# A written-down order for ScalarE, VectorE and GpSimd in the up phase of a decoder trunk

## The chip, the core and the metric

The kernel runs on one core of a Trainium2 chip. The metric is the device time of one execution in microseconds (us). The engines are PE (TensorE), ACT (ScalarE), DVE (VectorE), POOL (GpSimd) and SP (SyncE, which here only issues transfers). Each engine works through its own list of instructions in the list's order; an instruction whose inputs are not there holds up all that stand behind it.

## The reference

Two layers; each has a mixer and then an MLP. The change lies in the MLP, of which this is the whole (all float32, 1024 positions, width 1024, `D_FF` 4096):

```python
h = rms_norm(x, norm2[l])
x = x + jnp.square(jax.nn.relu(h @ w_up[l])) @ w_down[l]
```

## The kernel before, in words

Positions lie along the free axis in two halves of 512 (`c` 1 and 0), channels along the 128 partitions. A float32 operand is split into a high part, rounded to `fp32r` (`split`: a cast on ACT, line 131), and a low rest (a subtraction on DVE, line 132); each product is three matmuls of 128x512 (`mm3`, lines 219, 224, 225).

Both matrix products of the MLP use a Winograd form of Strassen's scheme on 2x2 blocks: 7 block products in place of 8. The table `STEPS` names them in order; the operands are sums of blocks, and the results are sums of products that gather in PSUM:

```python
STEPS = (
    ("X", 0, "A11", "B11"), ("Y", 0, "A12", "B21"), ("X", 1, "S2", "T2"), ("Z", 0, "S1", "T1"),
    ("X", 2, "S3", "T3"), ("Z", 1, "S4", "B22"), ("X", 3, "A22", "T4"),
)
```

The **up phase** (before: lines 931 to 1025) runs 16 times per layer (`fp`), each time over two tiles of 128 hidden channels; such a time is called a round here. A round has the seven steps 0 to 6; a step is 12 matmuls (4 pairs of input tiles, three each). Bank X takes four products one after the other, bank Z two, bank Y one.

Around the steps of a round, three kinds of work stand on the other engines:

- **Results.** After X0, X1 and Z0 ACT copies the bank to SBUF (`keep`, line 952: P1, U2, P5); the next product into the same bank may only start when that copy is done. DVE then forms each hidden block from those (B11 after step 1, line 998; B22 after step 4, line 1006; B12 after step 5, line 1010; B21 straight from PSUM after step 6), with a ReLU and the scale of the RMS norm (line 957). POOL squares it (line 960). B11 and B21 are split in two and stored; DVE forms T1 to T4 (line 972) from the blocks, which are stored whole.
- **The next round's weights** (`weight_steps`, lines 780 to 825). SP loads two tiles of 128x1024, a top and a low one, into the two buffers `raw` (line 801). The top one is split to A11 and A12. POOL forms s1 and s2 (lines 809, 810) into the tile `s`, which is split to S1 and S2; then s3 (line 818, split to S3), and s4, written into the low tile (line 820), which is split to S4 and A22. So the low buffer comes free for the next load only when that last split (`vh`, `vl`) is done. The split tiles have two buffers for `w` (A11 with A12, S1 with S2, in turn), and one each for `u` (S3) and `v` (S4 with A22).
- **Stores** of the hidden blocks to DRAM, issued by SP.

The kernel records all this in program order, and a scheduler then sets the order of each engine's list by priority and by its own idea of when things are ready; the results' work is recorded with a raised priority (`early(EVAC_EARLY)`). The 12 matmuls of a step are held in order by order-only dependences (`pace`). The **down phase** (from line 1050) has the same steps for `w_down`, and takes its weights by the same function.

Of the kernel before, what the change touches and what calls it, by code (L numbers as in the profile page):

```python
# [79 lines left out]
def trunk_kernel(tc, xT, w_in, w_out, w_up, w_down, pool_w, sgw, sgb, sgn, cst, outT):  # L80
# [8 lines left out]
    with ExitStack() as ctx:  # L89
# [23 lines left out]
        def tmp():  # L113
            return t512("tmp", 4)
# [12 lines left out]
        def early(n):  # L127
            return tc.high_priority(offset=n)

        def split(hi, lo, src):  # L130
            nc.scalar.copy(hi, src)  # L131
            nc.vector.tensor_sub(lo, src, hi.bitcast(F32))  # L132

        def xt(part, k, c, dt=F32R):

# [167 lines left out]
        for l in range(DEPTH):  # L303
# [476 lines left out]
            def weight_steps(srcs, n, out):  # L780

                turns = "p (n k w) -> p k n w"
                r = {}

                def room(tag, names, pool, bufs, by=None):
                    two = [
                        pool.tile([P, CH * len(names)], F32R, tag=tag + x, name=nm(tag + x), bufs=bufs) for x in "hl"
                    ]  # L790
                    for i, b in enumerate(names):
                        out[b] = tuple(
                            t.rearrange(by or "p (k n w) -> p k n w", n=n, k=len(names))[:, i] for t in two
                        )
# [10 lines left out]
                def top():  # L805
                    split(*room("w", ("A11", "A12"), per, 2, turns), r["top"])
                    s12 = r["s12"] = ex.tile([P, D], F32, tag="s", name=nm("s12"), bufs=1)
                    s1, s2 = (s12[:, i * CH : (i + 1) * CH].rearrange("p (n w) -> p n w", n=n) for i in range(2))
                    nc.gpsimd.tensor_add(s1, r["a2"][:, 0], r["a2"][:, 1])  # L809
                    nc.gpsimd.tensor_sub(s2, s1, r["a1"][:, 0])  # L810
                    r["s2"] = s2

                def sums():
                    split(*room("w", ("S1", "S2"), per, 2), r["s12"])

                def third():
                    s3 = tmp()
                    nc.gpsimd.tensor_sub(s3.rearrange("p (n w) -> p n w", n=n), r["a1"][:, 0], r["a2"][:, 0])
                    split(*room("u", ("S3",), mw, 1), s3)
                    nc.gpsimd.tensor_sub(r["a2"][:, 0], r["s2"], r["a1"][:, 1])  # L820

                def low():
                    split(*room("v", ("S4", "A22"), mw, 1, turns), r["low"])

                return {0: load, 2: top, 3: sums, 4: third, 6: low}

            def up_blocks(fp):

# [85 lines left out]
            def load_block(fp, b):  # L914

                h, lo = block_tiles(b)
                if b in STORED:
                    nc.sync.dma_start(h.bitcast(F32), hid[fp, b + "h"])
                    nc.sync.dma_start(lo.bitcast(F32), hid[fp, b + "l"])
                else:  # L920
                    raw = t512("hr", 4, F32, mw)
                    nc.sync.dma_start(raw, hid[fp, b])
                    split(h, lo, raw)
                return h, lo

            a_next = {}
            for _, step in sorted(weight_steps(*up_blocks(0), a_next).items()):
                step()


            with tc.tile_pool(name=f"mu{l}", bufs=1, reuse_waits="tile") as mu:

                rms_done = False

                def ct(dt=F32):
                    return t512("ct", 10, dt, mu)

                for fp in range(NFP):
                    a, a_next = a_next, {}
                    steps_w = weight_steps(*(up_blocks(fp + 1) if fp < NFP - 1 else down_blocks(0, 0)), a_next)  # L940
# [8 lines left out]

                    def keep(ps):  # L950
                        t = ct()
                        nc.scalar.copy(t, ps)  # L952
                        return t

                    def hidden(b, src, t, c):

                        nc.vector.scalar_tensor_tensor(  # L957
                            out=t, in0=src, scalar=0.0, in1=rbc[c], op0=ALU.max, op1=ALU.mult
                        )
                        nc.gpsimd.tensor_mul(t, t, t)  # L960
                        hb[b] = t
                        if b in STORED:
                            parts = [ct(F32R) for _ in range(2)]
                            split(*parts, t)
                            for x, part in zip("hl", parts):
                                nc.sync.dma_start(hid[fp, b + x], part.bitcast(F32))
                        elif classic or b != "B12":
                            nc.sync.dma_start(hid[fp, b], t)

                    def mixed(b, x, y, op):  # L970
                        t = ct()
                        op(t, hb[x], hb[y])  # L972
                        hb[b] = t
                        nc.sync.dma_start(hid[fp, b], t)

# [9 lines left out]
                    for step in range(len(STEPS)):  # L985
                        bank, i = products(a, xb, banks, step, 0)
                        ps = banks[bank]
                        if step == 3 and fp == 0:
                            rms(1, 0)
                            rms_done = True  # L990
                            for f, args in later:
                                f(*args)
                        with early(EVAC_EARLY):
                            if (bank, i) == ("X", 0):
                                kept["P1"] = keep(ps)
                            elif bank == "Y":
                                t = kept["P1"]
                                nc.vector.tensor_add(t, ps, t)
                                after_rms(hidden, "B11", t, t, 1)
                            elif (bank, i) == ("X", 1):  # L1000
                                kept["U2"] = keep(ps)
                            elif (bank, i) == ("Z", 0):
                                kept["P5"] = keep(ps)
                            elif (bank, i) == ("X", 2):
                                t = kept["P5"]
                                nc.vector.tensor_sub(t, ps, t)
                                hidden("B22", t, t, 0)
                            elif (bank, i) == ("Z", 1):
                                t = kept["U2"]
                                nc.vector.tensor_sub(t, t, ps)  # L1010
                                hidden("B12", t, t, 0)
                                if not classic:
                                    mixed("T1", "B11", "B12", nc.vector.tensor_sub)
                                    mixed("T2", "B22", "T1", nc.vector.tensor_add)
                                    mixed("T3", "B22", "B12", nc.vector.tensor_sub)
                            else:
                                hidden("B21", ps, ct(), 1)
                                if not classic:
# [31 lines left out]
            with tc.tile_pool(name=f"md{l}", bufs=1, reuse_waits="tile") as md:  # L1050
# [13 lines left out]
                for g in range(n_groups):  # L1064
                    bs, b_next = b_next, [{}, {}]
                    for u in range(2):
                        a, a_next, steps_w = a_next, {}, {}
                        if u == 0:
                            steps_w = weight_steps(*down_blocks(g, 1), a_next)
                        elif g < n_groups - 1:  # L1070
                            steps_w = weight_steps(*down_blocks(g + 1, 0), a_next)
                        banks = [{"X": pso(), "Y": psj(), "Z": psg()} for _ in range(2)]
                        for step in range(len(STEPS)):
                            for q in range(2):
# [3 lines left out]
                                with early(EVAC_EARLY):  # L1078
# [14 lines left out]
                            if step in steps_w:  # L1093
                                steps_w[step]()
# [125 lines left out]
```

## Time and profile before

| | |
|---|---|
| median of 3 runs (lowest to highest) | 2456.49 us (2449.84 to 2456.86) |
| the profiled execution: its own time | 2451.93 us |
| its span (first to last instruction) | 2450.2 us |
| mean granted clock of TensorE | 0.953 of full |
| up phase, first layer | about 505 to 905 us of the span |
| up phase, second layer | about 1709 to 2110 us |
| chain that ended last, by engine | PE 52%, DVE 14%, POOL 14%, issue 10%, DMA 5%, ACT 4% |

Times in the profile are counted from the span's start. A timeline row has the start, the duration, the engine, the line, the operation with the tile written and the tiles read, and in brackets the idle time of the engine before it with what ended that idle time. Matmuls overlap: the distance from one start to the next is what one costs, not its duration. On DVE and ACT, too, an instruction starts up to 0.1 us before the one ahead has its end recorded, so a run of them is read from start to start.

### The profile page before, as it was taken

To read this page: it belongs to the slowest core of one execution; us is meant where nothing else is said; L and a number is where in the kernel's file an instruction comes from. 1 tells how busy PE (TensorE), PEld (TensorE's weight loads), DVE (VectorE), ACT (ScalarE), POOL (GpSimd) and SP (SyncE) were. 2 spreads that over 40 slices of the span, in tenths; PEclk is the share of its full clock that TensorE was granted. 3 is DMA by queue.
4 is the path that set the end of the run, shared out by engine and by line. 5 is a ranking of instruction groups with operands and counts; after the bars stand their busy time and mean duration, and the time that the engine had idled before them with its cause. 6 is when DMAs were issued, how large, how long until landed. Compare 5 with 4: busy or idle time off the path is not lost.

```text
span 2450.2 us, 30479 instructions
## 1 busy us (share of the span) xinstructions
PE 2206.1 (90%) x10480; PEld 1817.2 (74%) x10480; DVE 1824.8 (74%) x2244; ACT 942.3 (38%) x1667; POOL 1263.6 (52%) x1169
## 2 busy tenths in 40 slices
PE   7999899878888889999999898997788888999997
PEld 5988787656666767888788887876666666778786
DVE  8787779956565669888868787798556665898874
ACT  5565553522222233333355665344222222333321
POOL 7676756754444442332367777459444454333315
PEclk9999899989999999999999998998899999999998
DMA  3000102234344367555311010232444343955421
GB/s 121 26 27 27 40 31 95 98 122 151 137 142 138 126 236 252 181 168 159 99 49 44 9 54 14 61 104 99 146 136 135 129 142 135 311 182 177 160 93 69
DMA packets 153739, 283.19 MB, mean 116 GB/s; under 512 B 15088, under 2 KB 48368, under 8 KB 153584
## 3 DMA queue, kind: packets, MB, share of 16 engines
q1 hardware_dynamic: 151920, 279.15, 34.4%
q10 hardware_dynamic: 1664, 2.10, 0.2%
q8 instruction: 82, 1.34, 0.2%
q14 instruction: 73, 0.60, 0.1%
HBM read 190.49 MB, written 90.70 MB: 115 GB/s over the span
## 4 chain that ended last, share of the span: by engine, by line
PE 52%; DVE 14%; POOL 14%; issue 10%; DMA 5%; ACT 4%; SPq 0%; DVEq 0%; POOLq 0%; ACTq 0%
PE po L219 8%; PE po L224 7%; PE po L225 7%; PE pj L219 5%; PE pj L224 5%; PE pj L225 5%; PE pg L219 3%; POOL s L809 3%; PE pg L225 3%; PE pg L224 3%; POOL s L810 3%; DVE s L411 3%; DMA raw<-in_w_up 2%; PE t L432 2%; POOL a L414 1%
## 5 line engine op out<-in xcount | busy, mean ns | idle before, releaser
L960 POOL TENSOR_TENSOR ct<-ct 128x512 f32<-128x512 f32 x128 | 137.9, 1077 | 387.3 <-DVE ct L957 386.3
L809 POOL TENSOR_TENSOR s<-raw 128x512 f32<-128x512 f32 x62 | 112.3, 1811 | 410.5 <-DMA raw<-in_w_down 244.3
L132 DVE TENSOR_TENSOR wl<-raw,wh 128x1024 fp32r<-128x1024 f32 x114 | 168.2, 1475 | 101.7 <-ACT wh L131 101.4
L414 POOL TENSOR_TENSOR a<-a,s 128x255 f32<-128x255 f32 (+1 forms) x192 | 220.6, 1151 | 29.4 <-DVE s L411 22.0
L131 ACT CAST wh<-raw 128x1024 fp32r<-128x1024 f32 x114 | 119.4, 1047 | 239.6 <-PE pj L224 217.1
L219 PE MATMUL pj<-hB,wh 128*128 128x512 f32 x504 | 198.1, 393 | 1.7 <-ACT hB L854 1.7
L224 PE MATMUL pj<-lB,wh 128*128 128x512 f32 x504 | 198.2, 393 | 1.0 <-DVE lB L855 1.0
L225 PE MATMUL pj<-hB,wl 128*128 128x512 f32 x504 | 197.6, 392 | 0.0
L219 PE MATMUL po<-hT,wh 128*128 128x512 f32 x256 | 117.4, 459 | 60.3 <-ACT ct L952 59.5
L411 DVE TENSOR_TENSOR_SCAN s<-s 128x256 f32<-128x256 f32 (+3 forms) x128 | 130.6, 1028 | 54.4 <-POOL s L404 52.8
L219 PE MATMUL po<-hT,uh 128*128 128x512 f32 x248 | 109.7, 442 | 66.1 <-ACT ct L952 62.2
L1056 DVE TENSOR_TENSOR acc<-acc,po 128x512 f32<-128x512 f32 x240 | 158.9, 678 | 11.4 <-PE po L225 10.2
L131 ACT CAST vh<-raw 128x1024 fp32r<-128x1024 f32 x62 | 65.1, 1049 | 233.7 <-PE po L224 172.4
L132 DVE TENSOR_TENSOR ct<-ct,ct 128x512 fp32r<-128x512 f32 x64 | 75.9, 1186 | 82.4 <-ACT ct L131 82.3
L972 DVE TENSOR_TENSOR ct<-ct,ct 128x512 f32<-128x512 f32 x120 | 110.2, 939 | 34.4 <-POOL ct L960 34.4
L131 ACT CAST ct<-ct 128x512 fp32r<-128x512 f32 x64 | 39.4, 615 | 228.3 <-POOL ct L960 228.3
L132 DVE TENSOR_TENSOR wl<-s,wh 128x1024 fp32r<-128x1024 f32 x62 | 83.2, 1341 | 51.9 <-ACT wh L131 51.9
L438 DVE TENSOR_TENSOR tl<-t,th 128x512 fp32r<-128x512 f32 (+1 forms) x160 | 98.1, 626 | 30.8 <-ACT th L436 29.7
L219 PEld LDWEIGHTS po<-hT,wh 128*128 128x128 f32 x256 | 54.8, 214 | 89.4 <-ACT ct L952 71.9
L219 PEld LDWEIGHTS po<-hT,uh 128*128 128x128 f32 x248 | 50.7, 205 | 92.7 <-ACT ct L952 75.3
L131 ACT CAST hT<-hr 128x512 fp32r<-128x512 f32 x122 | 74.0, 620 | 116.9 <-DMA hr<-hd_T 71.6
L400 ACT ACTIVATE s<-z 128x256 f32<-128x256 f32 (+1 forms) x192 | 94.5, 501 | 60.3 <-PE z L396 37.0
(270 smaller groups left out, 7396.6 us busy)
## 6 DMA issues: line engine op xcount, KB each, us to landing
raw<-in_w_up SPq DMA_DIRECT2D x64, 512.0 KB, 3.7
raw<-in_w_down SPq DMA_DIRECT2D x64, 512.0 KB, 3.7
hd_T<-ct SPq DMA_DIRECT2D x120, 256.0 KB, 4.0
hr<-hd_T SPq DMA_DIRECT2D x120, 256.0 KB, 3.3
raw<-in_w_in SPq DMA_DIRECT2D x36, 512.0 KB, 3.6
hd_B<-ct SPq DMA_DIRECT2D x34, 256.0 KB, 2.0
hr<-hd_B SPq DMA_DIRECT2D x34, 256.0 KB, 3.6
raw<-in_w_out SPq DMA_DIRECT2D x16, 512.0 KB, 3.6
```

Of the source, the lines that this page charges most:

```text
L131: nc.scalar.copy(hi, src)
L132: nc.vector.tensor_sub(lo, src, hi.bitcast(F32))
L219: mm = nc.tensor.matmul(ps, ah, bh, start=first and i == 0, stop=False, skip_group_check=more)
L224: nc.tensor.matmul(ps, ah, bl, start=False, stop=False, skip_group_check=more)
L225: mm = nc.tensor.matmul(ps, al, bh, start=False, stop=last and i == n - 1, skip_group_check=more)
L411: nc.vector.tensor_tensor_scan(sl, sl, sl, 1.0 if prev is None else prev[:, CH - 1 : CH], ALU.mult, ALU.bypass)
L414: nc.gpsimd.tensor_mul(a[:, lo + 1 : CH], a[:, lo + 1 : CH], s[:, lo : CH - 1])
L438: nc.vector.tensor_sub(tl[:, 0:wd], pt[:, 0:wd], th[:, 0:wd].bitcast(F32))
L809: nc.gpsimd.tensor_add(s1, r["a2"][:, 0], r["a2"][:, 1])
L960: nc.gpsimd.tensor_mul(t, t, t)
L972: op(t, hb[x], hb[y])
L1056: (nc.vector.tensor_add if sign > 0 else nc.vector.tensor_sub)(x, x, ps)
```

## The change

A helper `queue(engine, op)` keeps the last instruction it was given for each of ACT, DVE and POOL, and adds a dependence of the new one on it that only sets the order (no semaphore). It is on from the first round of each layer's up phase to its end. Every `keep`, split, sum, ReLU, square and mixed block of the phase goes through it, so that the three lists stand in the order in which the code names the operations. That order is new too. The tables `UP_AT` and `DOWN_AT` say after which step each part of the weights' work stands; 7 and 8 mean steps 0 and 1 of the next round. POOL's s4 stands right behind s3, no longer behind the split of S3. The splits of B11 and B21 are moved behind the copy of U2 and into the next round. PE's instructions, the arithmetic, and the buffers stay.

```diff
+        def queue(eng, op):
+            if queues[0] is not None:
+                if eng in queues[0]:
+                    tc.add_manual_dep(
+                        op.ins, queues[0][eng], mybir.DependencyInfo(NOSYNC, mybir.DependencyReason.DATA), reason="queue"
+                    )
+                queues[0][eng] = op.ins.name
...
-                return {0: load, 2: top, 3: sums, 4: third, 6: low}
...
+            UP_AT = {"load": 2, "A1": 3, "s1_s2": 3, "s3_s4": 4, "S12": 5, "S3": 7, "S4": 8}
+            DOWN_AT = {"load": 0, "A1": 2, "s1_s2": 2, "S12": 3, "s3_s4": 4, "S3": 4, "S4": 6}
...
+                    work = weight_steps(*(up_blocks(fp + 1) if fp < NFP - 1 else down_blocks(0, 0)), a_next)
+                    todo = {k - 7: v for k, v in left.items() if k > 6}
+                    for name, f in work.items():
+                        todo.setdefault(UP_AT[name], []).append(f)
+                    left = todo
...
+                    def in_two(fp, b, t):
+                        parts = [ct(F32R) for _ in range(2)]
+                        split(*parts, t)
+                        for x, part in zip("hl", parts):
+                            nc.sync.dma_start(hid[fp, b + x], part.bitcast(F32))
...
                             elif (bank, i) == ("X", 1):
                                 kept["U2"] = keep(ps)
+                                after_rms(in_two, fp, "B11", kept["P1"])
...
                             else:
-                                hidden("B21", ps, ct(), 1)
-                                if not classic:
-                                    mixed("T4", "B21", "T2", nc.vector.tensor_sub)
-                        if step in steps_w:
-                            steps_w[step]()
+                                relu("B21", ps, ct(), 1)
+                                left.setdefault(7, []).append(lambda fp=fp, t=hb["B21"]: in_two(fp, "B21", t))
+                        for f in todo.get(step, []):
+                            f()
+                        if not classic:
+                            if step == 5:
+                                mixed("T1", "B11", "B12", nc.vector.tensor_sub)
+                                mixed("T2", "B22", "T1", nc.vector.tensor_add)
+                                mixed("T3", "B22", "B12", nc.vector.tensor_sub)
+                            elif step == 6:
+                                mixed("T4", "B21", "T2", nc.vector.tensor_sub)
                         if fp == NFP - 1:
                             for p in range(2):
-                                b = STEPS[step][3]
-                                b_next[p][b] = load_block(p, b)
+                                b_next[p][b] = load_block(p, b, raws[p])
```

In the last round the transfers of the down phase's first blocks are issued at the start of each step (`raw_block`), and their splits stand in the queues too.

**ACT, one round of the first layer in the middle of the phase, before.** Rows name the tile written, then the tile read; `ct` from `po` or `pg` is a `keep`, `ct` from `ct` the high part of a hidden block, `wh`, `uh` and `vh` those of the weights. Here: B21's high part, P1, B11's high part, U2, S1 with S2, P5, S3, S4 with A22.

```order
L131 CAST ct_1342_6718<-ct_1341_6715 128x512
L952 COPY ct_1350_6746<-po_1347_6731 128x512
L131 CAST ct_1353_6767<-ct_1350_6746 128x512
L952 COPY ct_1355_6785<-po_1347_6731 128x512
L131 CAST wh_1360_6808<-s12_1358_6791 128x1024
L952 COPY ct_1359_6806<-pg_1349_6733 128x512
L131 CAST uh_1363_6830<-tmp_1362_6828 128x512
L131 CAST vh_1372_6883<-raw_1352_6750 128x1024
```

Behind the change, from P1 on (A11 with A12 is in it, the last row but one):

```order
L981 COPY ct_1344_6732<-po_1341_6717 128x512
L142 CAST uh_1345_6734<-tmp_1333_6668 128x512
L142 CAST ct_1347_6738<-ct_1339_6711 128x512
L142 CAST vh_1349_6759<-raw_1328_6629 128x1024
L981 COPY ct_1351_6775<-po_1341_6717 128x512
L142 CAST ct_1352_6777<-ct_1344_6732 128x512
L981 COPY ct_1356_6799<-pg_1343_6719 128x512
L142 CAST wh_1357_6801<-raw_1354_6783 128x1024
L142 CAST wh_1361_6842<-s12_1359_6805 128x1024
```

The copy of U2 stood behind the high part of B11 and stands ahead of it now; the splits of S3, B21 and S4 have come between P1 and U2.

**POOL, a round, before** (s1, s3, s2, s4, and the squares of B11, B22, B12, B21):

```order
L809 TENSOR_TENSOR s12_1331_6635<-raw_1325_6594 128x512
L818 TENSOR_TENSOR tmp_1335_6672<-raw_1324_6592,raw_1325_6594 128x512
L810 TENSOR_TENSOR s12_1331_6635<-s12_1331_6635,raw_1324_6592 128x512
L820 TENSOR_TENSOR raw_1325_6594<-s12_1331_6635,raw_1324_6592 128x4x128
L960 TENSOR_TENSOR ct_1323_6590<-ct_1323_6590 128x512
L960 TENSOR_TENSOR ct_1332_6650<-ct_1332_6650 128x512
L960 TENSOR_TENSOR ct_1328_6629<-ct_1328_6629 128x512
L960 TENSOR_TENSOR ct_1341_6715<-ct_1341_6715 128x512
```

and now (s1, s2, the square of B22, s3, s4, the squares of B12, B21, B11):

```order
L819 TENSOR_TENSOR s12_1332_6649<-raw_1328_6629 128x512
L820 TENSOR_TENSOR s12_1332_6649<-s12_1332_6649,raw_1327_6627 128x512
L990 TENSOR_TENSOR ct_1329_6643<-ct_1329_6643 128x512
L826 TENSOR_TENSOR tmp_1333_6668<-raw_1327_6627,raw_1328_6629 128x512
L827 TENSOR_TENSOR raw_1328_6629<-s12_1332_6649,raw_1327_6627 128x4x128
L990 TENSOR_TENSOR ct_1324_6619<-ct_1324_6619 128x512
L990 TENSOR_TENSOR ct_1339_6711<-ct_1339_6711 128x512
L990 TENSOR_TENSOR ct_1344_6732<-ct_1344_6732 128x512
```

The square of B22 stands between the weights' sums now, the squares of B12 and B21 stand behind all four of them, and that of B11 comes last before the next s1.

**DVE, from T1 on, before** (T1, low part of S4 with A22, T2, T3, ReLU of B21, low part of A11 with A12, of B21, T4, and the sum and the ReLU of B11):

```order
L972 TENSOR_TENSOR ct_1338_6694<-ct_1323_6590,ct_1328_6629 128x512
L132 TENSOR_TENSOR vl_1346_6728<-raw_1325_6594,vh_1345_6727 128x1024
L972 TENSOR_TENSOR ct_1339_6697<-ct_1332_6650,ct_1338_6694 128x512
L972 TENSOR_TENSOR ct_1340_6700<-ct_1332_6650,ct_1328_6629 128x512
L957 SCALAR_TENSOR_TENSOR ct_1341_6715<-po_1320_6575,rbc_1138_5541 128x512
L132 TENSOR_TENSOR wl_1357_6788<-raw_1351_6748,wh_1356_6787 128x1024
L132 TENSOR_TENSOR ct_1343_6719<-ct_1341_6715,ct_1342_6718 128x512
L972 TENSOR_TENSOR ct_1344_6724<-ct_1341_6715,ct_1339_6697 128x512
L998 TENSOR_TENSOR ct_1350_6746<-pj_1348_6732,ct_1350_6746 128x512
L957 SCALAR_TENSOR_TENSOR ct_1350_6746<-ct_1350_6746,rbc_1138_5541 128x512
```

and now (T1, T2, T3, ReLU of B21, T4, low parts of S3 and of B21, sum and ReLU of B11, low part of S4 with A22):

```order
L1002 TENSOR_TENSOR ct_1336_6690<-ct_1317_6576,ct_1324_6619 128x512
L1002 TENSOR_TENSOR ct_1337_6693<-ct_1329_6643,ct_1336_6690 128x512
L1002 TENSOR_TENSOR ct_1338_6696<-ct_1329_6643,ct_1324_6619 128x512
L987 SCALAR_TENSOR_TENSOR ct_1339_6711<-po_1314_6561,rbc_1135_5534 128x512
L1002 TENSOR_TENSOR ct_1340_6714<-ct_1339_6711,ct_1337_6693 128x512
L143 TENSOR_TENSOR ul_1346_6735<-tmp_1333_6668,uh_1345_6734 128x512
L143 TENSOR_TENSOR ct_1348_6739<-ct_1339_6711,ct_1347_6738 128x512
L1031 TENSOR_TENSOR ct_1344_6732<-pj_1342_6718,ct_1344_6732 128x512
L987 SCALAR_TENSOR_TENSOR ct_1344_6732<-ct_1344_6732,rbc_1135_5534 128x512
L143 TENSOR_TENSOR vl_1350_6760<-raw_1328_6629,vh_1349_6759 128x1024
```

The low part of S4, behind which the low weight buffer comes free, stood second and stands last of these ten. On SP's list the load into that buffer follows the two stores of B21, where a store of a T block stood ahead of it.

## Rows read from the trace of the kernel before

**Rows 1.** Page, part 1: span; busy time and its share, by engine.
```profile
span 2450.2 us, 30479 instructions
...
PE 2206.1 (90%) x10480; PEld 1817.2 (74%) x10480; DVE 1824.8 (74%) x2244; ACT 942.3 (38%) x1667; POOL 1263.6 (52%) x1169
```

**Rows 2.** Waits of PE, 560 to 860 us: total us, times, longest us.
```profile
PE po L219 <- ACT ct L952: 43.8, 23, 2.8
```

**Rows 3.** Timeline, PE, second layer's up phase: start us, us, engine, line, op.
```profile
1737.20 0.50 PE L219 MATMUL po<-hT,wh 128*128 128x512 f32 x1 [1.91 <-ACT ct L952]
...
1745.95 0.50 PE L219 MATMUL po<-hT,uh 128*128 128x512 f32 x1 [2.90 <-ACT ct L952]
...
1748.57 0.63 PE L225 MATMUL po<-hT,ul 128*128 128x512 f32 x1
1749.00 0.63 PE L219 MATMUL po<-hT,uh 128*128 128x512 f32 x1
...
1753.16 0.40 PE L219 MATMUL po<-hT,vh 128*128 128x512 f32 x1
...
1758.67 0.39 PE L219 MATMUL pj<-hB,wh 128*128 128x512 f32 x1
```

**Rows 4.** Timeline, ACT, the same stretch.
```profile
1755.94 1.05 ACT L131 CAST vh<-raw 128x1024 fp32r<-128x1024 f32 x1 [5.22 <-PE po L224]
...
1770.95 0.62 ACT L131 CAST ct<-ct 128x512 fp32r<-128x512 f32 x1 [7.54 <-POOL ct L960]
1771.47 0.58 ACT L952 COPY ct<-po 128x512 f32<-128x512 f32 x1
...
1780.49 1.05 ACT L131 CAST vh<-raw 128x1024 fp32r<-128x1024 f32 x1 [4.88 <-PE po L224]
```

**Rows 5.** Timeline, POOL, the same stretch.
```profile
1760.13 1.04 POOL L960 TENSOR_TENSOR ct<-ct 128x512 f32<-128x512 f32 x1 [4.24 <-DVE ct L957]
1762.44 2.39 POOL L809 TENSOR_TENSOR s<-raw 128x512 f32<-128x512 f32 x1 [1.27 <-ACT wh L131]
1764.79 1.72 POOL L818 TENSOR_TENSOR tmp<-raw,raw 128x512 f32<-128x512 f32 x1
1766.47 1.74 POOL L810 TENSOR_TENSOR s<-s,raw 128x512 f32<-128x512 f32 x1
1768.30 1.62 POOL L820 TENSOR_TENSOR raw<-s,raw 128x512 f32<-128x512 f32 x1
1769.88 1.03 POOL L960 TENSOR_TENSOR ct<-ct 128x512 f32<-128x512 f32 x1
```

**Rows 6.** Timeline, DVE, the same stretch.
```profile
1757.02 1.23 DVE L132 TENSOR_TENSOR vl<-raw,vh 128x1024 fp32r<-128x1024 f32 x1 [0.40 <-ACT vh L131]
1758.16 1.29 DVE L972 TENSOR_TENSOR ct<-ct,ct 128x512 f32<-128x512 f32 x2
1759.37 0.68 DVE L957 SCALAR_TENSOR_TENSOR ct<-po,rbc 128x512 f32<-128x512 f32 x1
1762.44 1.23 DVE L132 TENSOR_TENSOR wl<-raw,wh 128x1024 fp32r<-128x1024 f32 x1 [2.39 <-ACT wh L131]
1763.58 1.80 DVE L132 TENSOR_TENSOR ct<-ct,ct 128x512 fp32r<-128x512 f32 x1
...
1766.99 0.68 DVE L998 TENSOR_TENSOR ct<-pj,ct 128x512 f32<-128x512 f32 x1
1767.70 1.06 DVE L957 SCALAR_TENSOR_TENSOR ct<-ct,rbc 128x512 f32<-128x512 f32 x1
```

**Rows 7.** Timeline, SP's queue, the same stretch.
```profile
1758.27 0.33 SPq L801 DMA_DIRECT2D raw<-in_w_up  x1
```

**Rows 8.** Chain that ended last, by time: start us, us, what.
```profile
1762.44 2.39 POOL s L809
...
2063.54 2.39 POOL s L809
```

**Rows 9.** Line 809: count, then ns shortest/median/longest, first and last start.
```profile
L809 POOL TENSOR_TENSOR s<-raw x62: 1276/1770/2391, 468.7 to 2349.2; 128x512 f32<-128x512 f32 x62
```

More of the change, by code (lines that the diff above doesn't have):

```diff
@@ L128, in early @@
             return tc.high_priority(offset=n)
+        queues = [None]
+        def queue(eng, op):
[5 more added lines that the diff above has]
+                queues[0][eng] = op.ins.name
         def split(hi, lo, src):
-            nc.scalar.copy(hi, src)
-            nc.vector.tensor_sub(lo, src, hi.bitcast(F32))
+            queue("act", nc.scalar.copy(hi, src))
+            queue("dve", nc.vector.tensor_sub(lo, src, hi.bitcast(F32)))
         def xt(part, k, c, dt=F32R):
@@ L803, in load, with s1_s2 @@
                     r["a1"], r["a2"] = (x.rearrange(turns, n=n, k=2) for x in raws)
-                def top():
-                    split(*room("w", ("A11", "A12"), per, 2, turns), r["top"])
+                def s1_s2():
                     s12 = r["s12"] = ex.tile([P, D], F32, tag="s", name=nm("s12"), bufs=1)
                     s1, s2 = (s12[:, i * CH : (i + 1) * CH].rearrange("p (n w) -> p n w", n=n) for i in range(2))
-                    nc.gpsimd.tensor_add(s1, r["a2"][:, 0], r["a2"][:, 1])
-                    nc.gpsimd.tensor_sub(s2, s1, r["a1"][:, 0])
+                    queue("pool", nc.gpsimd.tensor_add(s1, r["a2"][:, 0], r["a2"][:, 1]))
+                    queue("pool", nc.gpsimd.tensor_sub(s2, s1, r["a1"][:, 0]))
@@ L811, in top @@
                     r["s2"] = s2
[L813 to L823, printed above, removed]
@@ L825, in weight_steps, with s3_s4 @@
-                return {0: load, 2: top, 3: sums, 4: third, 6: low}
+                def s3_s4():
+                    s3 = r["s3"] = tmp()
+                    s3 = s3.rearrange("p (n w) -> p n w", n=n)
+                    queue("pool", nc.gpsimd.tensor_sub(s3, r["a1"][:, 0], r["a2"][:, 0]))
+                    queue("pool", nc.gpsimd.tensor_sub(r["a2"][:, 0], r["s2"], r["a1"][:, 1]))
+                return {
+                    "load": load,
+                    "A1": lambda: split(*room("w", ("A11", "A12"), per, 2, turns), r["top"]),
+                    "s1_s2": s1_s2,
+                    "S12": lambda: split(*room("w", ("S1", "S2"), per, 2), r["s12"]),
+                    "s3_s4": s3_s4,
+                    "S3": lambda: split(*room("u", ("S3",), mw, 1), r["s3"]),
+                    "S4": lambda: split(*room("v", ("S4", "A22"), mw, 1, turns), r["low"]),
+                }
@@ L912, in load_acc, with raw_block, load_block @@
                 nc.sync.dma_start(acc_[m, c], xmid[m, c])
-            def load_block(fp, b):
+            def raw_block(fp, b):
+                if b in STORED:
+                    return None
+                raw = t512("hr", 4, F32, mw)
+                nc.sync.dma_start(raw, hid[fp, b])
+                return raw
+            def load_block(fp, b, raw=None):
                 h, lo = block_tiles(b)
@@ L920, in load_block @@
                 else:
-                    raw = t512("hr", 4, F32, mw)
-                    nc.sync.dma_start(raw, hid[fp, b])
-                    split(h, lo, raw)
+                    split(h, lo, raw or raw_block(fp, b))
                 return h, lo
             a_next = {}
-            for _, step in sorted(weight_steps(*up_blocks(0), a_next).items()):
+            for step in weight_steps(*up_blocks(0), a_next).values():
                 step()
@@ L951, in keep, with relu @@
                         t = ct()
-                        nc.scalar.copy(t, ps)
+                        queue("act", nc.scalar.copy(t, ps))
                         return t
-                    def hidden(b, src, t, c):
-                        nc.vector.scalar_tensor_tensor(
+                    def relu(b, src, t, c):
+                        hb[b] = t
+                        queue("dve", nc.vector.scalar_tensor_tensor(
                             out=t, in0=src, scalar=0.0, in1=rbc[c], op0=ALU.max, op1=ALU.mult
[L959 to L967, printed above, removed]
-                            nc.sync.dma_start(hid[fp, b], t)
+                        ))
+                        queue("pool", nc.gpsimd.tensor_mul(t, t, t))
+                        if b not in STORED and (classic or b != "B12"):
+                            nc.sync.dma_start(hid[fp, b], t)
+                    def in_two(fp, b, t):
[3 more added lines that the diff above has]
+                            nc.sync.dma_start(hid[fp, b + x], part.bitcast(F32))
                     def mixed(b, x, y, op):
                         t = ct()
-                        op(t, hb[x], hb[y])
+                        queue("dve", op(t, hb[x], hb[y]))
                         hb[b] = t
@@ L987, in trunk_kernel @@
                         ps = banks[bank]
+                        b = STEPS[step][3]
+                        if fp == NFP - 1:
+                            raws = [raw_block(p, b) for p in range(2)]
                         if step == 3 and fp == 0:
@@ L1005, in trunk_kernel @@
                                 t = kept["P5"]
-                                nc.vector.tensor_sub(t, ps, t)
-                                hidden("B22", t, t, 0)
+                                queue("dve", nc.vector.tensor_sub(t, ps, t))
+                                relu("B22", t, t, 0)
                             elif (bank, i) == ("Z", 1):
                                 t = kept["U2"]
-                                nc.vector.tensor_sub(t, t, ps)
-                                hidden("B12", t, t, 0)
@@ L1025, in trunk_kernel @@
-                                b_next[p][b] = load_block(p, b)
+                                b_next[p][b] = load_block(p, b, raws[p])
+                for k in sorted(left):
+                    if k > 6:
+                        for f in left[k]:
+                            f()
+                queues[0] = None
             def finish(c, t, n, parts):
@@ L1092, in trunk_kernel @@
                                         add_to(m0 + 2, 1, ps, 1)
-                            if step in steps_w:
-                                steps_w[step]()
+                            for name, f in work.items():
+                                if DOWN_AT[name] == step:
+                                    f()
                             if g < n_groups - 1:
```

19 lines of the change are left out of this document (9 added, 10 removed).

## The prediction

> **What bounds the kernel now.** I read the page first: PE is busy 90% of a span of 2450.2 us [rows 1], so an order can only win where PE waits. The waits of PE come next: for 300 us in the first layer's up phase they are one thing, a matmul on bank X that waits for ACT's `keep` [rows 2]. The timeline of one round shows where: X1 starts after 1.91 us of idling (for P1), X2 after 2.90 us (for U2) [rows 3]. At full clock PE does not need that time: from the first matmul of X3 to the first of Y0 are 24 matmuls in 1758.67 - 1753.16 = 5.51 us, 0.2296 us each [rows 3], so the 84 of a round take 19.3 us. A round lasts longer. Between the starts of line 809 at 1762.44 and 2063.54 lie twelve rounds, hence 301.1 / 12 = 25.1 us for one [rows 8].
>
> Why 25.1? The chain goes round in a circle, and each link has a row. The split of S4 and A22 on ACT starts at 1755.94, when X3 has ended [rows 4]; its low part on DVE runs 1757.02 to 1758.25 [rows 6]; the freed buffer's load is issued at 1758.27 [rows 7]; s1 starts at 1762.44, 4.19 us after the low part's end; the four POOL sums take until 1769.88, and the square of B11 ends at 1770.91 [rows 5]; ACT casts B11 at 1770.95 and copies U2, which stands behind it, at 1771.47 [rows 4]. X2 waits for that copy; X2, Z1 and X3 (36 matmuls, 8.3 us) follow, and ACT's next S4 split starts at 1780.49 [rows 4]. That is 24.55 us round the circle. The rest to 25.1 is TensorE's clock: behind the wait for U2 some matmuls of X2 stand 0.43 us apart (1748.57 to 1749.00) in place of 0.23 [rows 3], its 1.2 GHz level, and X2 lies on the circle.
>
> **The change, part by part.** It adds no instruction to an engine and takes none away. It cuts this circle at U2, whose copy now stands ahead of B11's cast, and it takes PE out of it. What is late next? The low weight buffer is still one of a kind: it must be loaded, summed and split before the next load. In the new lists these links follow each other, all by rows of the round above:
>
> - Low part of S4 done, to s1: **4.19 us** (1758.25 to 1762.44) [rows 5, 6]. The load now follows the two stores of B21 on SP, not one of T1; the cost of that is unknown, and I take none (bound below: nothing; above: half a load, 2 us, were it to share the engines with them).
> - POOL: s1, s2, B22's square, s3, s4, B12's square. The four sums took 1769.88 - 1762.44 = 7.44 us, a square 1.04 [rows 5]: **9.52 us**. The square of B22 is ready, as its ReLU needs only X2. The bounds for the four sums are those of line 809 alone, 1.28 and 2.39 us [rows 9], so 5.1 to 9.6 us; I keep 7.44, because DVE has sums and splits beside them in the new order too.
> - DVE: T1 needs B12's square (0.08 us, the step from the ReLU's end at 1760.05 to the square at 1760.13 [rows 5, 6]). T1, T2, T3 at 0.6 each (two in 1.21, from 1758.16 to 1759.37): 1.8. ReLU of B21 with that step 0.76, its square on POOL 1.04, a step back 0.08. T4, low part of S3, low part of B21 at 0.6: 1.8. Sum of B11 0.71 (1766.99 to 1767.70), ReLU 0.6, low part of S4 1.23 [rows 5, 6]. With the first step: **8.1 us**. The sum of B11 needs Y0, which ends some 5.5 us after X3; by then DVE is no further than that, so this asks no more of PE.
>
> Sum: 4.19 + 9.52 + 8.1 = **21.8 us** a round, above PE's 19.3, below today's 25.1. So PE still waits, 2.5 us a round in all in place of 4.8, but it no longer carries the circle, and what its clock loses falls into that slack. ACT's casts of B21 and S4 hide beside DVE's T4 to B11 sum; without that cover they would add their 1.6 us.
>
> One place turns on DVE and POOL getting in each other's way. When DVE's low part of A11 and POOL's s1 both start at 1762.44, DVE takes its plain 1.23 and POOL 2.39; the next DVE split, started at 1763.58 with s1 still at work, takes 1.80 in place of the 0.68 of undisturbed 512-wide ones [rows 5, 6]. So one waits for the other. In the new order the low part of S4 and the square of B11 become ready together, with DVE ahead by about 0.1 us, since POOL must be told of the ReLU's end. The Trainium skill, "SBUF — State Buffer", Who interferes with whom, says that the pair of ports they share is locked for a whole instruction by whichever came first. Those rows agree; by that rule the low part keeps 1.23 us, while by an even sharing it would take up to 2.27 and the round 22.8.
>
> Gain: 25.1 - 21.8 = 3.3 us a round. I count 14 rounds a layer, leaving out the first, where the results wait for the RMS norm, and the last, where the down phase's blocks come in: 28 x 3.3 = 92 us. The other phases keep their work, and I give them nothing; their lists move in places, which I bound at 10 us either way, three rounds' gain. From the profiled execution's 2451.9 us that makes **2360 us**. That execution lies 4.6 us under the median of the runs, inside their spread of 7.
>
> **The rivals.**
>
> - *PE becomes the bound.* If POOL's four sums fall where DVE leaves them alone, they take 5.1 us [rows 9], the round is 19.5, and the gain 28 x 5.6 = 157: 2295 us. Against it: A11's low part, two sums, two ReLUs and S12's low part on DVE lie in those same microseconds. Chance 0.07.
> - *The load comes late.* Behind the two stores of B21 it takes 2 us more, the round 23.8, the gain 36: 2416 us. For it: the load is all on the new circle and nothing can hide it. Against it: a store of 256 KB stood shortly ahead of it before as well. Chance 0.09.
> - *The clock takes it back.* PE's remaining waits lie behind two copies (U2, P5). If after each some eight matmuls run at 0.43, that is 2 x 1.6 us, and PE's own round 19.3 + 2.5 + 3.2 = 25.0: no change, 2449 us. It decides only if PE's delays reach DVE, so if Y0 ends after B21's split is done; the waits would shrink first. [...] Chance 0.04.
> - *Slower, by the lock.* T1 to T4 and the low parts of S3 and B21 now lie on the circle. If each meets a POOL instruction and takes 1.8 in place of 0.68 [rows 6], the round grows by 6 x 1.1 to 28.4, and the kernel by 92: 2544 us. It is slower from the third such meeting on (25.1 is passed at 3.3 us). Against it: POOL has only squares to do then, and waits for the load. Chance 0.05.
>
> That the change does nothing is out: the lists differ at the places shown above.
>
> **How the numbers follow.** The forecast has the remaining chance, 0.75. Its bounds are the POOL sums': 19.5 to 23.9 us a round, 2295 to 2418 us; the range takes the upper end, and as the lower one 2323 us, at 20.5 us a round, halfway from 21.8 to PE's limit. Below it lie most of the first rival and some of the forecast, above it the last two. About 0.3% (7 us) is what a measurement tells from no change here. The forecast and the first two rivals are faster by more: 0.91; the third is no change: 0.04; the fourth is slower: 0.05.
>
> **What would show it.** Right: rounds of about 22 us between starts of s1 in both layers; s1 waiting for the load of the low buffer, and POOL's squares of B22 and B12 behind it; X2 no longer waiting 2.9 us; U2 copied ahead of B11's cast; the granted clock in the up phase up. Wrong: rounds of 19.5 (PE's waits gone), DVE's T blocks at 1.8 us, a load that lands 6 us after its issue, or rounds of 22 with the gain lost in the last round or the down phase.

## The result, and the profile after

The changed kernel takes **2332.03 us** (median of 4 runs, 2331.14 to 2337.33) against 2454.89 us for the kernel before on the same chip: a ratio of 0.951, interval 0.949 to 0.953. The range held the time; the forecast of 2360 us gave the change 92 us. The profiled execution of the changed kernel (span 2329.5 us) is 120.7 us shorter than that of before [rows 1]. Its page's lines:

```profile
span 2329.5 us, 30444 instructions
...
PE 2159.5 (93%) x10480; PEld 1776.2 (76%) x10480; DVE 1776.4 (76%) x2244; ACT 943.5 (41%) x1667; POOL 1283.3 (55%) x1169
```

PE's busy time fell by 47 us though it does the same matmuls: fewer of them run at 1.2 GHz, and the mean granted clock rose from 0.953 to 0.975. The first layer's up phase, before and after, in stretches of time (columns: length; busy us and instructions of PE, PEld, DVE, ACT, POOL; granted clock; DMA share; GB/s):

```profile
505.00:905.00 400.00, 334.44 (x1318) 262.02 (x1317) 240.49 (x269) 102.40 (x149) 177.36 (x126) 0.93 0.43 148
```

```profile
505.00:850.00 345.00, 318.95 (x1352) 248.57 (x1351) 217.72 (x272) 103.57 (x151) 190.30 (x126) 1.00 0.49 172
```

The granted clock went from 0.93 to 1.00. Where the time went shows by landmarks that both kernels have: the first and the last ReLU of B11, B22 and B12 in a layer's up phase, and the last sum from PSUM in its down phase. Of these lines, the instruction count, then shortest, median and longest ns, then first and last start. Before:

```profile
L957 DVE SCALAR_TENSOR_TENSOR ct<-ct,rbc x48: 682/692/1761, 509.5 to 904.9; 128x512 f32<-128x512 f32 x48
...
L957 DVE SCALAR_TENSOR_TENSOR ct<-ct,rbc x48: 682/692/1084, 1714.1 to 2106.1; 128x512 f32<-128x512 f32 x48
...
L1056 DVE TENSOR_TENSOR acc<-acc,po x128: 670/676/690, 910.8 to 1231.6; 128x512 f32<-128x512 f32 x128
...
L1056 DVE TENSOR_TENSOR acc<-acc,po x112: 672/676/690, 2110.5 to 2386.5; 128x512 f32<-128x512 f32 x112
```

After:

```profile
L987 DVE SCALAR_TENSOR_TENSOR ct<-ct,rbc x48: 680/1078/1103, 509.8 to 849.6; 128x512 f32<-128x512 f32 x48
...
L987 DVE SCALAR_TENSOR_TENSOR ct<-ct,rbc x48: 682/1075/1525, 1646.7 to 1984.3; 128x512 f32<-128x512 f32 x48
...
L1096 DVE TENSOR_TENSOR acc<-acc,po x128: 673/680/690, 841.8 to 1171.8; 128x512 f32<-128x512 f32 x128
...
L1096 DVE TENSOR_TENSOR acc<-acc,po x112: 672/680/693, 1977.0 to 2265.3; 128x512 f32<-128x512 f32 x112
```

| stretch | before, us | after, us | difference |
|---|---|---|---|
| up phase, layer 0 (first to last ReLU) | 395.4 | 339.8 | -55.6 |
| down phase, layer 0 (to the last sum) | 326.7 | 322.2 | -4.5 |
| layer 1's mixer (to the next first ReLU) | 482.5 | 474.9 | -7.6 |
| up phase, layer 1 | 392.0 | 337.6 | -54.4 |
| down phase, layer 1 | 280.4 | 281.0 | +0.6 |

So 110.0 of the 120.7 us come from the two up phases. The start before the first ReLU and the end after the last sum changed by 0.3 and 0.5 us.

**The round.** Between these two starts of s1 lie thirteen rounds (POOL's timeline):

```profile
535.30 1.42 POOL L819 TENSOR_TENSOR s<-raw 128x512 f32<-128x512 f32 x1 [3.10 <-DMA raw<-in_w_up]
...
812.61 1.70 POOL L819 TENSOR_TENSOR s<-raw 128x512 f32<-128x512 f32 x1 [2.82 <-DMA raw<-in_w_up]
```

277.3 / 13 = 21.3 us a round; the forecast was 21.8, and it was 25.1 before [rows 8]. The links of the forecast circle stand in the round from 658 to 681 us. DVE, from the low part of S4 to the next:

```profile
658.16 1.22 DVE L143 TENSOR_TENSOR vl<-raw,vh 128x1024 fp32r<-128x1024 f32 x1
...
672.60 2.02 DVE L1002 TENSOR_TENSOR ct<-ct,ct 128x512 f32<-128x512 f32 x3 [3.56 <-POOL ct L990]
...
676.38 0.69 DVE L1002 TENSOR_TENSOR ct<-ct,ct 128x512 f32<-128x512 f32 x1 [1.16 <-POOL ct L990]
...
679.52 1.22 DVE L143 TENSOR_TENSOR vl<-raw,vh 128x1024 fp32r<-128x1024 f32 x1
```

POOL, from B11's square to B21's square:

```profile
658.38 1.90 POOL L990 TENSOR_TENSOR ct<-ct 128x512 f32<-128x512 f32 x1 [3.39 <-issue]
663.14 1.66 POOL L819 TENSOR_TENSOR s<-raw 128x512 f32<-128x512 f32 x1 [2.86 <-DMA raw<-in_w_up]
664.88 1.63 POOL L820 TENSOR_TENSOR s<-s,raw 128x512 f32<-128x512 f32 x1
666.48 1.48 POOL L990 TENSOR_TENSOR ct<-ct 128x512 f32<-128x512 f32 x1
667.92 2.27 POOL L826 TENSOR_TENSOR tmp<-raw,raw 128x512 f32<-128x512 f32 x1
670.27 1.30 POOL L827 TENSOR_TENSOR raw<-s,raw 128x512 f32<-128x512 f32 x1
671.52 1.05 POOL L990 TENSOR_TENSOR ct<-ct 128x512 f32<-128x512 f32 x1
675.30 1.04 POOL L990 TENSOR_TENSOR ct<-ct 128x512 f32<-128x512 f32 x1 [2.73 <-DVE ct L987]
```

The low buffer comes free at 659.38. SP issues its load at once, and s1 waits for that until 663.14, 3.76 us later (in before 4.19 [rows 5, 6]):

```profile
659.41 0.33 SPq L812 DMA_DIRECT2D raw<-in_w_up  x1
```

From the issue to the landing of this one load, in the changed kernel and then in before (the load issued at 1758.27 [rows 7]):

```profile
DMA to landing us min/median/max: 3.6/3.6/3.6
...
DMA to landing us min/median/max: 4.0/4.0/4.0
```

The six POOL instructions from s1 to B12's square end at 672.57, 9.43 us. DVE's T1 starts at 672.60, its low part of S4 ends at 680.74, 8.14 us after that. 3.76 + 9.43 + 0.03 + 8.14 = 21.36: the circle closes, and each link waits for the one ahead of it (the bracket at 672.60 names POOL, that at 663.14 the load).

PE's waits from 540 to 800 us, in the middle of the phase (total us, times, longest), and ACT around the copies of U2 (677.85) and P5 (682.19):

```profile
PE pg L230 <- ACT ct L981: 15.8, 12, 1.3
```

```profile
677.85 0.58 ACT L981 COPY ct<-po 128x512 f32<-128x512 f32 x1
681.67 0.62 ACT L142 CAST ct<-ct 128x512 fp32r<-128x512 f32 x1 [3.24 <-POOL ct L990]
682.19 0.58 ACT L981 COPY ct<-pg 128x512 f32<-128x512 f32 x1
```

This is the only wait listed. X2's wait for U2, 2.90 us in the round shown before [rows 3], is gone; U2 is copied ahead of B11's cast. What is left is Z1's wait for P5, 1.3 us a round, because P5 stands behind B11's cast.

### The profile page after: what moved, and what is told of

Read it like the earlier page. It is cut to its first block, busy times and chain, and to the rows that moved or that the text cites. A ratio compares the mean times of both kernels' runs of the same rounds, so it can differ in the third digit from the quotient of the medians.

```text
span 2329.5 us, 30444 instructions
## 1 busy us (share of the span) xinstructions
PE 2159.5 (93%) x10480; PEld 1776.2 (76%) x10480; DVE 1776.4 (76%) x2244; ACT 943.5 (41%) x1667; POOL 1283.3 (55%) x1169
## 5 line engine op out<-in xcount | busy, mean ns | idle before, releaser
L819 POOL TENSOR_TENSOR s<-raw 128x512 f32<-128x512 f32 x62 | 98.6, 1591 | 452.2 <-DMA raw<-in_w_down 275.7
L990 POOL TENSOR_TENSOR ct<-ct 128x512 f32<-128x512 f32 x128 | 174.5, 1363 | 208.1 <-DVE ct L987 109.7
L1002 DVE TENSOR_TENSOR ct<-ct,ct 128x512 f32<-128x512 f32 x120 | 80.4, 690 | 134.5 <-POOL ct L990 133.5
L142 ACT CAST wh<-s 128x1024 fp32r<-128x1024 f32 x62 | 65.1, 1050 | 204.7 <-POOL s L820 194.4
L230 PE MATMUL pg<-hB,vh 128*128 128x512 f32 x240 | 98.1, 409 | 37.1 <-ACT ct L981 36.9
L143 DVE TENSOR_TENSOR wl<-s,wh 128x1024 fp32r<-128x1024 f32 x62 | 90.9, 1466 | 40.1 <-ACT wh L142 40.1
L826 POOL TENSOR_TENSOR tmp<-raw,raw 128x512 f32<-128x512 f32 x62 | 120.3, 1941 | 0.0
L230 PE MATMUL po<-hT,wh 128*128 128x512 f32 x256 | 105.7, 413 | 8.3 <-ACT ct L981 4.0
L230 PEld LDWEIGHTS pj<-hB,wh 128*128 128x128 f32 x504 | 95.2, 189 | 21.9 <-ACT hB L871 2.5
L235 PEld LDWEIGHTS pj<-lB,wh 128*128 128x128 f32 x504 | 95.1, 189 | 21.4 <-DVE lB L872 1.6
```

What stands on the lines that cost most here:

```text
L142: queue("act", nc.scalar.copy(hi, src))
L143: queue("dve", nc.vector.tensor_sub(lo, src, hi.bitcast(F32)))
L230: mm = nc.tensor.matmul(ps, ah, bh, start=first and i == 0, stop=False, skip_group_check=more)
L235: nc.tensor.matmul(ps, ah, bl, start=False, stop=False, skip_group_check=more)
L819: queue("pool", nc.gpsimd.tensor_add(s1, r["a2"][:, 0], r["a2"][:, 1]))
L826: queue("pool", nc.gpsimd.tensor_sub(s3, r["a1"][:, 0], r["a2"][:, 0]))
```

## The experiments

Each is measured against the kernel before, run on the same chip; for e5 and e6 that is another chip than for e1 to e4 (before took 2453.13 us there, and 2450.78 us here). Rounds are counted as above, thirteen in the first layer.

**e1: the changed code without the dependences.** Is it the written order itself, or the new places in the code?

```diff
-                queues[0] = {}
+                queues[0] = None
```

> The changed kernel without its order-only dependences: the code stands as changed (U2's copy recorded ahead of B11's cast, the weights' parts at their new steps), the scheduler sets the lists. Theory: what counts is that PE is off the circle, which the new place of B11's split does by itself; the lists will differ from the written ones, so some of the gain goes: rounds of 21.5 to 23 us, 2335 to 2390 us. Rival (the dependences do it; without them the scheduler goes back to its old lists): rounds of about 25 us, 2440 to 2460 us.

Measured: 2368.15 us, ratio 0.966 (0.964 to 0.968). POOL's starts of s1:

```profile
530.41 2.21 POOL L819 TENSOR_TENSOR s<-raw 128x512 f32<-128x512 f32 x1 [1.50 <-DMA raw<-in_w_up]
...
822.14 2.25 POOL L819 TENSOR_TENSOR s<-raw 128x512 f32<-128x512 f32 x1 [1.36 <-DMA raw<-in_w_up]
```

22.4 us a round. PE now waits for copies twice a round:

```profile
PE po L230 <- ACT ct L981: 15.3, 11, 1.4
PE pg L230 <- ACT ct L981: 13.3, 11, 1.4
```

So the new places in the code alone bring 83 us. By the landmarks (first to last ReLU) the up phases took 352.7 and 349.5 us: 85 of the 110 us that the change saves there come from the new places, and the dependences, which hold the lists to them, bring the other 25. The rival was half right: in a round from the middle of the phase the scheduler gave POOL its old list back (s1, s3, s2, s4, then the four squares), but U2's copy stayed ahead of B11's cast.

**e2: the kernel before, with U2 ahead of B11's cast, and nothing else in the edit.** This cuts the old circle at the place where the prediction said it closes.

```diff
                         if b in STORED:
-                            parts = [ct(F32R) for _ in range(2)]
-                            split(*parts, t)
-                            for x, part in zip("hl", parts):
-                                nc.sync.dma_start(hid[fp, b + x], part.bitcast(F32))
+                            if b != "B11":
+                                in_two(b, t)
...
                                 kept["U2"] = keep(ps)
+                                behind[0] = copied[0]
+                                after_rms(in_two, "B11", kept["P1"])
+                                behind[0] = None
```

(`in_two` holds the four lines taken out, and `split` makes its cast depend, by order alone, on the instruction named in `behind`.)

> The kernel before, with one thing changed: the split of B11 is recorded behind the copy of U2 and its cast is held behind that copy by an order-only dependence; all other lists are the scheduler's. Theory: the old circle is cut at U2; X2 stops waiting 2.9 us, the wait of X1 for P1 (1.9 us) stays, rounds of 22 to 23.5 us, 2365 to 2405 us. Rival (the gain comes from the whole written order, not from this cut): rounds of 24.5 us or more, 2430 to 2460 us.

Measured: 2383.64 us, ratio 0.973 (0.971 to 0.975). Starts of s1, 22.9 us a round, and PE's waits in the round around 670 us:

```profile
531.01 2.22 POOL L815 TENSOR_TENSOR s<-raw 128x512 f32<-128x512 f32 x1 [1.47 <-DMA raw<-in_w_up]
...
828.21 2.23 POOL L815 TENSOR_TENSOR s<-raw 128x512 f32<-128x512 f32 x1 [1.42 <-DMA raw<-in_w_up]
```

```profile
669.26 0.50 PE L225 MATMUL po<-hT,wh 128*128 128x512 f32 x1 [1.91 <-ACT ct L958]
...
678.87 0.50 PE L225 MATMUL pg<-hB,vh 128*128 128x512 f32 x1 [0.97 <-ACT ct L958]
```

X1 still waits 1.91 us for P1, as in before [rows 3]; X2 no longer waits. In a round from the middle of the phase the lists of DVE and POOL are those of before, and ACT's differs in this one place. It carries 67 us, more than half of the change (in the up phases, 72 of the 110 us).

**e3: the low buffer freed earlier.** The circle that the prediction found for the changed kernel runs through the release of the low weight buffer. The split of S4 needs nothing from T4, B21's split or B11, so it can stand ahead of them.

```diff
-            UP_AT = {"load": 2, "A1": 3, "s1_s2": 3, "s3_s4": 4, "S12": 5, "S3": 7, "S4": 8}
+            UP_AT = {"load": 2, "A1": 3, "s1_s2": 3, "s3_s4": 4, "S12": 5, "S3": 7, "S4": 6}
```

> The changed kernel with the split of S4 and A22 two places earlier (step 6, behind the ReLU of B21, ahead of T4): UP_AT of S4 is 6, not 8. Theory: the new circle runs through the release of the low weight buffer; T4, S3's and B21's low parts, B11's sum and ReLU (3.4 us and a square's wait of 1.1) leave it, so it falls to about 17 us and something else bounds the round (PE's 19.3 and its waits): rounds of 19.5 to 21 us, 2280 to 2325 us. Rival (DVE's or PE's own work bounds the round at 21.3, the buffer only seems to): unchanged, 2325 to 2340 us.

Measured: 2317.82 us, ratio 0.945 (0.944 to 0.947). Starts of s1:

```profile
531.93 1.31 POOL L819 TENSOR_TENSOR s<-raw 128x512 f32<-128x512 f32 x1
...
799.95 1.31 POOL L819 TENSOR_TENSOR s<-raw 128x512 f32<-128x512 f32 x1
```

20.6 us a round; s1 no longer waits for a load (no bracket). The circle is gone, and something else bounds the round, 1.3 us above PE's need; e4 looks for it.

**e4: A11's split behind B22's ReLU as well.** In e3 DVE's low part of A11 meets POOL's s2 (657.45 to 659.08; the expectation below says s1) and lasts 1.94 us, with B22's sum and ReLU behind it:

```profile
658.22 1.94 DVE L143 TENSOR_TENSOR wl<-raw,wh 128x1024 fp32r<-128x1024 f32 x1 [0.31 <-ACT wh L142]
```

```diff
-            UP_AT = {"load": 2, "A1": 3, "s1_s2": 3, "s3_s4": 4, "S12": 5, "S3": 7, "S4": 6}
+            UP_AT = {"load": 2, "A1": 4, "s1_s2": 3, "s3_s4": 4, "S12": 5, "S3": 7, "S4": 6}
```

> The kernel of e3_s4_step6 with, in addition, the split of A11 and A12 behind step 4 (behind the ReLU of B22) in place of step 3. Theory: once the buffer is off the circle, DVE's low part of A11, which waits for its cast and then meets POOL's s1, holds up the sums of B22 and B12; moved behind B22's ReLU it costs a step nothing: rounds of 19.3 to 20.5 us, 2255 to 2310 us, and below e3_s4_step6. Rival: A11's split is as much in the way one step later; the same as e3_s4_step6 within 7 us.

Measured: 2293.53 us, ratio 0.936 (0.934 to 0.937). Starts of s1, and the stretch from 540 to 780 us (columns as above):

```profile
530.98 1.31 POOL L819 TENSOR_TENSOR s<-raw 128x512 f32<-128x512 f32 x1
...
786.79 1.31 POOL L819 TENSOR_TENSOR s<-raw 128x512 f32<-128x512 f32 x1
```

```profile
540.00:780.00 240.00, 238.79 (x1027) 191.50 (x1026) 177.06 (x208) 77.25 (x111) 153.34 (x98) 1.00 0.51 177
```

19.7 us a round, with PE busy 238.8 of 240 us at a granted clock of 1.00: now PE bounds the phase, at what the prediction worked out as its need, 19.3 us, and a little.

**e5: the low buffer freed later.** The opposite dose of e3.

```diff
-            UP_AT = {"load": 2, "A1": 3, "s1_s2": 3, "s3_s4": 4, "S12": 5, "S3": 7, "S4": 8}
+            UP_AT = {"load": 2, "A1": 3, "s1_s2": 3, "s3_s4": 4, "S12": 5, "S3": 7, "S4": 9}
```

> The changed kernel with the split of S4 and A22 later: UP_AT of S4 is 9, not 8, so that on DVE it stands behind B11's low part, and on ACT behind the copy of U2 and B11's cast. Theory: the release of the low weight buffer is the circle, so a round grows by what the release loses: in the trace of the changed kernel B11's low part ends 2.3 us after the low part of S4 (661.66 against 659.38), and a low part of S4 behind it would end some 3.5 us later than now: rounds of 23.3 to 25 us, 2390 to 2440 us. Rival (the round is bound by the DVE's or PE's own work, the buffer has room): rounds stay at 21.3 to 21.8, 2328 to 2350 us.

Measured: 2400.98 us, ratio 0.979 (0.977 to 0.981). Starts of s1, 23.4 us a round, and DVE's T1 with the low part of S4 in one round:

```profile
536.78 1.61 POOL L819 TENSOR_TENSOR s<-raw 128x512 f32<-128x512 f32 x1 [6.53 <-DMA raw<-in_w_up]
...
841.07 1.31 POOL L819 TENSOR_TENSOR s<-raw 128x512 f32<-128x512 f32 x1 [6.64 <-DMA raw<-in_w_up]
```

```profile
662.16 2.02 DVE L1002 TENSOR_TENSOR ct<-ct,ct 128x512 f32<-128x512 f32 x3 [2.19 <-POOL ct L990]
...
671.91 1.23 DVE L143 TENSOR_TENSOR vl<-raw,vh 128x1024 fp32r<-128x1024 f32 x1 [0.25 <-ACT vh L142]
```

From T1 to the end of the low part are 10.98 us here (662.16 to 673.14), 2.84 more than in the changed kernel. The round grew by 2.1, since POOL's six instructions, from s1 at 653.64 to T1, ran 0.9 us shorter, with DVE less in their way. With e3 this shows that the release of the low buffer is on the circle.

**e6: the last round's block splits out of the queues.** From e4:

```diff
+                            held, queues[0] = queues[0], None
                             for p in range(2):
                                 b_next[p][b] = load_block(p, b, raws[p])
+                            queues[0] = held
```

> The kernel of e4_s4_step6_a1_step4 with the last round's block splits (load_block) left out of the queues, so that the scheduler places them. Theory: in the last round ACT stands 9.5 and 6.6 us at the cast of a block whose transfer has not landed, with the next weights' casts behind it, and PE waits 9 us in all for those; free of the queue they cost little: 5 to 12 us a layer less, 2268 to 2284 us. Rival (the transfers themselves, at 0.9 to 1.05 of the engines' share there, bound that stretch): 2288 to 2299 us.

Measured: 2279.48 us, ratio 0.929 (0.928 to 0.931), the fastest of all, 2.3% under the changed kernel. In e4 ACT stood at two casts of blocks in the last round, 9.50 us at this one and 6.61 us at the one at 833.44:

```profile
820.11 1.28 ACT L142 CAST hT<-hr 128x512 fp32r<-128x512 f32 x2 [9.50 <-DMA hr<-hd_T]
```

By the landmarks the two up phases took 314.2 and 312.5 us in e4, and 304.9 and 307.3 in e6: 9.3 and 5.2 us less. But the first layer's down phase takes 6.7 us more in e6, so from the first ReLU to the last sum of its MLP only 2.6 us are left of the gain; in the second layer it is 6.5 us. Most of the rest lies where nothing was edited: layer 1's mixer takes 7.4 us less, with another list (see the last section), and the first ReLU of layer 0 comes 3.2 us later. So the time fell into the expected range in part by luck: the 5 to 12 us a layer show in the second layer alone.

## Why the prediction was right, and what it missed

- **What bounds the kernel before: right.** e2 cuts the circle at U2's copy and takes 67 us off, with everything else left to the scheduler.
- **PE's waits of 4.8 us a round: those of one kind of round.** The waits of before come to 43.8 us in twelve rounds, 3.65 us a round [rows 2]. X2 waits 2.8 us in some rounds and 1.25 in the others; the circle of 24.55 us that the forecast walked is a round of the second kind, and the 2.90 us are from the round ahead of it:

```profile
1772.10 0.50 PE L219 MATMUL po<-hT,uh 128*128 128x512 f32 x1 [1.25 <-ACT ct L952]
```

  Behind one of the two waits of a round, some eight matmuls mostly stand 0.43 us apart. Where they are X1's, the round takes 24.3 to 24.9 us, where they are X2's, 26.0 to 26.6 (two rounds, with a late load between them, took 25.5 and 25.3). Two rounds that follow each other, with the same waits (1.91 and 2.80 us), show what X2's cost: starts of s1, and the granted clock in 25 us of each (columns as above):

```profile
708.59 2.27 POOL L809 TENSOR_TENSOR s<-raw 128x512 f32<-128x512 f32 x1 [1.39 <-ACT wh L131]
733.03 2.39 POOL L809 TENSOR_TENSOR s<-raw 128x512 f32<-128x512 f32 x1 [1.27 <-ACT wh L131]
759.31 2.27 POOL L809 TENSOR_TENSOR s<-raw 128x512 f32<-128x512 f32 x1 [1.39 <-ACT wh L131]
```

```profile
705.00:730.00 25.00, 20.29 (x88) 16.00 (x87) 15.67 (x19) 6.25 (x9) 11.41 (x8) 1.00 0.41 139
730.00:755.00 25.00, 20.28 (x81) 15.79 (x80) 14.06 (x17) 6.26 (x9) 11.53 (x8) 0.93 0.40 135
```

  24.4 us with no slowed matmul, 26.3 with seven in X2. So the forecast was right that the rest from 24.55 to 25.1 us is the clock, and that X2 lies on the circle.
- **The new circle: right.** It is the one predicted, link by link: 3.76, 9.43 and 8.14 us against 4.19, 9.52 and 8.1. e3 and e5 move its last link both ways, and the round follows.
- **The load, 4.19 us: too long by 0.43.** Over 26 rounds that is 11 us. The bracket of s1 in before names ACT's cast of A11 [rows 5], but s1 did not wait for it: in the round that starts at 809.80 it started before that cast had ended. In both kernels s1 starts within 0.2 us of the load's landing, so the difference is the load's own, 4.0 us to landing in before and 3.6 here. In before, three stores of T blocks were issued close to it (1756.65, 1758.87 and 1759.48 against 1758.27); here the nearest stores are 2.5 us ahead and 1.6 us behind. That they make the difference was not tried. The forecast's upper bound, 2 us more behind B21's stores, did not come.
- **28 rounds of 3.3 us: the sum came out by other parts.** The thirteen rounds of each layer between starts of s1 (531.75 to 859.04 and 1736.15 to 2063.54 in before, 535.30 to 812.61 and 1671.87 to 1950.58 now) took 50.0 and 48.7 us less, 3.8 a round. The stretch from the first ReLU to the first of them lost 3.2 and 3.1 us, and the one from the last of them to the last ReLU gained 8.9 and 8.8. So the 26 rounds saved 98.7 us and the ends 11.4, where the forecast's count of 28 has 85.8 and 6.6. Why the ends changed was not followed up.
- **Nothing for the other phases: 11 us off.** 4.5 us in the first layer's down phase, whose weights' sums the change moves too, and 7.6 in layer 1's mixer, where no code changed but the scheduler's lists did. With the small rest they make 10.7 us, a little over the bound of 10. The mixer's part is no merit of the new order: the same stretch, with the same code, took 481.8 us in e1, 483.9 in e2, 480.3 in e3, 484.5 in e4, 480.8 in e5 and 477.1 in e6 (the last section says which lists these are).
- **Together:** 92 us, 13 for rounds that gained 3.8 us and not 3.3, 5 for the ends, 11 for the other phases, make 121 against 120.7.
- **POOL's four sums, 7.44 us by the rows of before: right together with the squares, by luck.** The six POOL instructions took 9.43 us, near the 9.52 of the forecast; but the sums took 6.94, half a microsecond less, and the two squares 2.49 in place of 2.08. Neither bound (5.1 or 9.6 for the sums) was near. So PE did not become the bound, as the first rival had it; it did in e4.
- **The lock: as the forecast chose.** DVE's low part of S4 started at 658.16 and took 1.22 us; POOL's square of B11 started at 658.38 and took 1.90 in place of 1.04. The one that came first was not slowed, as the Trainium skill, "SBUF — State Buffer", Who interferes with whom, says. The slower rival, by that lock, failed for the reason held against it: T1 to T3 took 2.02 us together, undisturbed, as POOL was idle beside them.
- **The clock: the third rival fell.** Waits of 1.3 us a round went with a granted clock of 1.00. In before, matmuls at 1.2 GHz behind X2's wait were on the circle (above), so the round gave back more than the waits: PE's listed waits fell from 3.65 to 1.3 us a round, and the round by 3.8. Not every wait is followed by them: in the round from 708.59 PE waited 1.91 and 2.80 us, and the granted clock from 705 to 730 us was 1.00.

## What to carry to other kernels

Where a phase repeats, follow the waits from one instruction until they return to it, and add up that circle's rows; the sum gives the period. First see whether all rounds are alike: here they were of two kinds. Cutting the circle at one place in one engine's list (e2) was worth more here than all the rest of the reordering. Before an order is fixed, look for the next circle, here a buffer of which there is only one, and put the instruction that frees it as early as its inputs allow (e3, then e4: 51 us less in the two up phases than with the change itself). Compare such kernels phase by phase with landmarks, since a scheduler may move lists in phases that nobody touched.

## What was not expected

Edits in the MLP changed the list that the scheduler made for the second layer's mixer, though not the first layer's. By the names in the traces, ACT, DVE and POOL have two lists in that stretch over the eight kernels, but for a few places. Before and e1 to e5 have the one and took 480.3 to 484.5 us; the changed kernel and e6 have the other and took 474.9 and 477.1. So the list is worth some 6 us, and one list differs by some 4 us between the executions profiled. In the 50 us that begin 100 us after the last sum of layer 0, the kernel before and the changed one show:

```profile
1331.60:1381.60 50.00, 46.20 (x291) 42.22 (x290) 40.62 (x56) 31.57 (x71) 34.66 (x51) 0.93 0.08 22
```

```profile
1271.80:1321.80 50.00, 47.26 (x310) 42.48 (x309) 44.69 (x60) 32.30 (x72) 41.40 (x54) 1.00 0.07 22
```

310 matmuls against 291, at a granted clock of 1.00 against 0.93. Which edit brings the other list was not tried; the dependences alone do not, since e3 to e5 have them and the old list.
